# Attention scores by half a chunk at once, with row-half products for the keys' low parts, in a one-core hybrid decoder layer

## The chip, the cores and the metric

The kernel runs on one core of a Trainium2 chip, as one launch. The metric is the device time of that launch in microseconds (us); lower is better. Engines are named as in the profile: PE (matrix products), PEld (its weight loads), DVE (vector), ACT (scalar functions), POOL (GpSimd), SP (issues DMA). PSUM is the memory that products are written to, in eight banks of 512 f32 per partition.

## What is computed

One layer over a new sequence of 4096 tokens and 64 sample tokens, width 1024, all in f32. The parts that matter here:

```python
z = rmsnorm(x, g_pre) @ w_in                       # cut into cb, cc, ch, cg, q, k, v, ag, mq, mg
out_a = silu(cg) * cb * conv3(cc * ch)             # 256 wide
out_b = silu(ag) * window_attention(q, k, v, sink) # 8 query heads, 2 key heads, head_dim 64, window 128
out_c = silu(mg) * attention(mq, mem_k, mem_v)     # 4 heads, head_dim 64, 256 memory tokens
y = concat(out_a, out_b, out_c) @ w_out
x = x + rmsnorm(y, g_post)
```

The window attention goes by blocks of 128 queries against 256 keys (the block before and its own), with one extra sink logit per head. The sample tokens do the same against caches.

## The kernel before

The layer runs in two stages. The first (`input_projection`, up to about 930 us) makes z by Strassen products (line 368) and writes queries, keys, values and gates to DRAM. The second stage computes attention and the output product; the change lies in it.

*High and low parts.* [...] A query tile `q` holds for each head 128 rows: 64 rows of high parts and 64 rows of low parts, in either order. A key tile `kst` holds the high parts of the keys in both halves of its rows (part 0) and the low parts in both halves (part 1). So one product of 128 rows with part 0 gives high x high + low x high, and a second one with part 1 gives the products with the keys' low parts. `mk` holds the memory's keys in the same way.

*Chunks, blocks and units.* Tokens go in 16 chunks of 256, of two 128-token blocks each. `Block.run` (line 1476) makes the output product of one block: two parts of 512 columns, each 8 k-tiles x 3 products (line 1492, tile `y`), so 48 products of 512 columns a block. `starts` names the k at which `start` (line 1525) is called between these products: four times a block from block 2 on, eight times in blocks 0 and 1. Each call puts one unit into PE's stream. A chunk has eight units: four window units (line 1237; one block of queries, one key head, four query heads) and four cross units (line 1174; one head, all 256 queries). Chunk 0 runs in the first stage; chunks 1 and 2 share blocks 0 and 1; from block 2 on a chunk takes two blocks.

*The course of a unit.* A window unit makes 16 score products (line 1246, tile `ws`), ACT copies one half of the scores out (1248), DVE copies the other under a mask (1249), finds maxima (1251), ACT makes exponentials and sums (1259), DVE divides (1264); two calls later PE transposes four heads (1269, tile `wt`), ACT copies them out (1271) and POOL masks them (1276, 1279). A cross unit makes 8 score products (1182, tile `xs`), a maximum (1183), exponentials (1186), one call later POOL multiplies by the reciprocal sums (1191), two calls later PE transposes (1197, tile `xt`) and DVE and ACT copy out one half each (1201). `Pipe.start` (1061) keeps these due times. One call after the transposes of a pair of units PE makes the value products (1088, 1218, 1224, tile `wo`), on column halves of the array and then on quarters of it, and DVE multiplies them into the gates (1227, 1170).

*What sets the order.* The order of this stage is not written out: a planner orders the instructions of each engine from the program's order and its own estimate of when their inputs are there. Each engine runs its queue in that order.

*PSUM.* The eight banks (line 1013) are two each for `s` (scores), `t` (transposes), `z` (y), and one tile of two banks for `pv` (values).

*Loads.* POOL issues four loads of keys (1110) and four of queries (1121) for a chunk, a chunk ahead; SP issues those of gates, x and results. `Block.split` (1460) makes high and low parts of the finished gates on ACT and DVE. Sample tokens are worked in between, in blocks 26 to 28 (`late_start`).

Of the kernel before, what the change touches and what calls it, by code (L numbers as in the profile page):

```python
# [52 lines left out]
def hybrid_layer(ctx: ExitStack, tc: tile.TileContext, a: dict):  # L53
# [951 lines left out]
    def open_attention():  # L1005
# [7 lines left out]
        ps = {tag: ctx.enter_context(tc.tile_pool(name=f"ps{tag}", bufs=1 if tag == "pv" else 2, space=bass.MemoryType.PSUM))  # L1013
              for tag in ("s", "t", "z", "pv")}
# [75 lines left out]
    class Chunk:  # L1090


        def __init__(self, c):
            self.c = c
            self.t0 = NS + CT * c
            self.ts = slice(self.t0, self.t0 + CT)
# [18 lines left out]
        def load_queries(self):  # L1115

            self.q = self.pool("q").tile([P, 12, CT], F32R, tag="q", name=f"q{self.c}")
            for part in range(2):
                for hh in range(2):
                    half = hh if part == 0 else 1 - hh  # L1120
                    G.dma_start(self.q[half * 64 : half * 64 + 64, hh::2, :],  # L1121
                                  qd[part, 1:7, hh * 64 : hh * 64 + 64, self.ts].rearrange("j p n -> p j n"))
# [34 lines left out]
        def cross_pair(self, j, band_values):  # L1157
# [4 lines left out]
            def both():  # L1162
                banks = ps["pv"].tile([P, 2, 512], F32, tag="pv", name=f"wo{c}_{j}") if c else None
# [10 lines left out]
        def cross_unit(self, h, pts):  # L1174
            c, nb = self.c, CT // P
            q = self.q[:, h]
            p = work([P, nb, 256], "p", f"xp{c}_{h}")
            mx, nm, den, rd = (tiny.tile([P, 4], F32, tag=n, name=f"x{n}{c}_{h}") for n in ("mx", "nm", "den", "rd"))
            s = psum("s", f"xs{c}_{h}").rearrange("p (b k) -> p b k", b=nb)
            for i in range(nb):  # L1180
                for part in range(2):
                    TE.matmul(s[:, i, :], q[:, i * P : i * P + P], third["mk"][:, part, h, :], start=part == 0, stop=part == 1)  # L1182
# [4 lines left out]
            V.reciprocal(rd[:, :nb], den[:, :nb])  # L1187
            yield 1
            for i in range(nb):

                G.tensor_scalar(p[:, i, :], p[:, i, :], rd[:, i : i + 1], 0.5, op0=ALU.mult, op1=ALU.mult)  # L1191
            yield 1
            pt = work([P, 2, CT], "xpt", f"xpt{c}_{h}")
            for kt in range(2):
                t = psum("t", f"xt{c}_{h}_{kt}")
# [9 lines left out]
        def window_pair(self, i):  # L1205
# [6 lines left out]
            def both_halves(o):  # L1212
                o = o.rearrange("p a (h q) -> p a h q", h=4)
                for n in range(2):
                    for kvh in range(2):
                        cs = slice(64 * kvh, 64 * kvh + 64)
                        v, p3 = steps[kvh][n]
                        TE.matmul(o[cs, n], v[:, cs], p3[:, :, 64 * n : 64 * n + 64], start=True, stop=False,  # L1218
                                  tile_position=(0, 64 * kvh))
                for n in range(2):  # L1220
                    for kvh in range(2):
                        cs, rs = slice(64 * kvh, 64 * kvh + 64), slice(64 - 64 * n, 128 - 64 * n)
                        v, p3 = steps[kvh][n]
                        TE.matmul(o[cs, 1 - n], v[rs, cs], p3[rs, :, 64 - 64 * n : 128 - 64 * n], start=False, stop=True,  # L1224
                                  tile_position=(64 - 64 * n, 64 * kvh))
                gate = self.mix[:, 4:8, i * P : i * P + P].rearrange("p h (a q) -> p a h q", a=2)
# [298 lines left out]
    def start():  # L1525
# [9 lines left out]
        if n == 0:  # L1535
            chunk_load(c + 1)
# [146 lines left out]
```

## Time and profile before

| what | value |
|---|---|
| median of 3 runs | 1536.71 us (1536.7 to 1536.77) |
| the profiled execution's own time | 1536.4 us |
| its span in the profile | 1534.7 us |
| PE busy | 1521.5 us |
| DVE, ACT, POOL busy | 1145.5, 805.7, 376.1 us |
| first y product, last y product start | 931.2 us, 1528.2 us |
| y products, records and mean length | 1560 of whole blocks, 388 to 399 ns |
| score products of windows (line 1246) | 512, 283 ns |
| transposes of windows (line 1269) | 256, 272 ns |

A record of a PE product lasts from its start to its modelled end. Products overlap in the array, so the pace is the distance from start to start, not the record's length, and a record longer than its usual length shows that the product stood waiting in the array, for its weights for example. The name before the arrow is the tile written, those after it are the tiles read; `128*64` is the part of the array that a product takes (rows times columns). An f32 value product appears as two records.

### The profile page before, as it was taken

Reading aid. Unit: us, or ns where it says so; the run is one execution under the profiler, and the core shown is the slowest. Engines: PE = TensorE matmul, PEld = TensorE weight load, DVE = VectorE, ACT = ScalarE, POOL = GpSimd, SP = SyncE. Lnnn points to the kernel's source line nnn. Section 1 sums busy time; section 2 is a strip of 40 time slices with the busy share of each in tenths; the row PEclk is TensorE's granted clock in tenths of the full one; section 3 lists DMA queues with packets and bytes.
Section 4 is the critical chain, followed back from the end, with each engine's and each line's share of the span. In section 5 each row is a group of like instructions: output and inputs, shape, how many; then the busy total and the mean of one; then the engine's idle time right before and its main releaser. Section 6 shows DMA issues by size and latency. Waiting matters only on the chain.

```text
span 1534.7 us, 30168 instructions
## 1 busy us (share of the span) xinstructions
PE 1521.5 (99%) x11341; PEld 1399.5 (91%) x11341; DVE 1145.5 (75%) x2055; ACT 805.7 (52%) x2039; POOL 376.1 (25%) x603
## 2 busy tenths in 40 slices
PE   9999999999999999999999999999999999999998
PEld 9999999999999999999999998788888888888877
DVE  6788887899988777897777678766666666666743
ACT  6675665475322222354454447655666556565632
POOL 0223332211300000000101203544444444444310
PEclk9999999999999999999999999999999999999999
DMA  9989999878855333677877789977777777777333
GB/s 265 194 222 225 283 284 266 272 242 298 193 181 180 126 126 126 220 230 280 227 273 230 229 293 254 231 161 153 156 148 148 151 162 149 158 160 150 130 110 96
DMA packets 177942, 306.28 MB, mean 200 GB/s; under 512 B 33925, under 2 KB 107653, under 8 KB 177765
## 3 DMA queue, kind: packets, MB, share of 16 engines
q1 hardware_dynamic: 130901, 227.38, 48.2%
q0 software_dynamic: 46176, 75.92, 25.5%
q8 instruction: 90, 1.47, 0.4%
q10 hardware_dynamic: 720, 1.05, 0.2%
q14 instruction: 55, 0.45, 0.1%
HBM read 197.23 MB, written 108.05 MB: 199 GB/s over the span
## 4 chain that ended last, share of the span: by engine, by line
PE 86%; DMA 7%; DVE 4%; issue 1%; ACT 1%; POOL 1%; SPq 0%; ACTq 0%; DVEq 0%; POOLq 0%
PE c L368 47%; PE y L1492 23%; PE ws L1246 4%; DMA nat<-in_x_p 3%; DMA md<-th 2%; PE wo L1088 2%; PE wt L1269 2%; PE xs L1182 2%; PE xt L1197 2%; PE wo L1218 2%; PE wo L1224 1%; PE mem_acc L789 1%; DMA qd<-z 1%; DVE z L375 1%; DMA xr<-in_x_p 0%
## 5 line engine op out<-in xcount | busy, mean ns | idle before, releaser
L1492 PE MATMUL y<-wo,mh 128*128 128x512 f32 (+1 forms) x1040 | 349.8, 399 | 0.0
L375 DVE TENSOR_TENSOR z<-c,z 128x520 f32<-128x520 f32 (+1 forms) x308 | 194.5, 646 | 79.2 <-PE c L368 78.2
L1492 PEld LDWEIGHTS y<-wo,mh 128*128 128x128 f32 x1040 | 194.3, 188 | 39.2 <-issue 2.4
L1492 PE MATMUL y<-wo,ml 128*128 128x512 f32 (+1 forms) x520 | 201.6, 388 | 0.0
L1259 ACT ACTIVATE sm<-sm,wnm 128x128 f32<-128x128 f32 x256 | 99.5, 390 | 61.0 <-DVE wnm L1253 60.2
L1191 POOL TENSOR_SCALAR xp<-xp,xrd 128x256 f32<-128x256 f32 x128 | 74.4, 588 | 209.6 <-DVE xrd L1187 209.6
L1492 PEld LDWEIGHTS y<-wo,ml 128*128 128x128 f32 x520 | 98.2, 189 | 16.3
L1183 DVE TENSOR_REDUCE xmx<-xs 128x2 f32<-128x512 f32 x64 | 44.1, 689 | 59.2 <-PE xs L1182 59.1
L1271 ACT COPY wpt<-wt 128x512 f32<-128x512 f32 x64 | 37.3, 582 | 88.1 <-PE wt L1269 85.6
L1246 PEld LDWEIGHTS ws<-kst,q 128*128 128x128 f32 x512 | 69.9, 190 | 5.3 <-ACT xp L1186 0.7
L1499 DVE TENSOR_TENSOR yn<-y,gpost 128x512 f32<-128x512 f32 (+1 forms) x66 | 45.1, 683 | 39.6 <-PE y L1492 39.3
L1246 PE MATMUL ws<-kst,q 128*128 128x256 f32 x512 | 73.0, 283 | 0.4 <-ACT xp L1186 0.4
L1500 ACT ACTIVATE y<-y 128x512 f32<-128x512 f32 (+1 forms) x66 | 38.6, 584 | 64.2 <-DVE yn L1499 64.2
L737 POOL CAST wmask<-negs 128x256 uint8<-128x256 f32 x1 | 0.9, 864 | 268.3 <-ACT z L377 268.3
L1279 POOL TENSOR_SCALAR_AFFINE_SELECT wpt<-wpt 128x512 f32<-128x512 f32 x64 | 52.7, 824 | 42.1 <-ACT wpt L1271 39.1
L1186 ACT ACTIVATE xp<-xs,xnm 128x256 f32<-128x256 f32 x128 | 58.8, 464 | 7.1 <-DVE xnm L1184 7.1
L1121 POOL DMA_DIRECT2D q<-qd x64 | 42.8, 674 | 70.6 <-DVE wo L186 60.9
L276 ACT ACTIVATE nat<-nat 104x1024 f32<-104x1024 f32 x40 | 42.3, 1057 | 26.1 <-DMA nat<-in_x_p 26.1
L1510 DVE SCALAR_TENSOR_TENSOR xr<-yn,yst,xr 128x1024 f32<-128x1024 f32 (+2 forms) x34 | 43.4, 1280 | 15.5 <-POOL yst L1506 13.2
L1110 POOL DMA_DIRECT2D kst<-qd x64 | 38.6, 616 | 63.5 <-PE xt L1197 41.4
L1249 DVE COPY_PREDICATED sm<-wmask,ws 128x256 f32<-128x256 uint8 x124 | 52.2, 437 | 2.5 <-ACT sm L1248 2.1
L1276 POOL TENSOR_SCALAR_AFFINE_SELECT wpv<-wpt 128x512 f32<-128x512 f32 x62 | 40.2, 648 | 50.6 <-ACT wpt L1271 50.5
(961 smaller groups left out, 5095.5 us busy)
## 6 DMA issues: line engine op xcount, KB each, us to landing
q<-qd POOLq DMA_DIRECT2D x64, 384.0 KB, 7.9
xr<-in_x_p SPq DMA_DIRECT2D x32, 512.0 KB
nat<-in_x_p SPq DMA_DIRECT2D x39, 416.0 KB
o_yp<-xr SPq DMA_DIRECT2D x31, 512.0 KB
md<-th POOLq DMA_DIRECT2D x48, 260.0 KB, 7.9
qd<-zh SPq DMA_DIRECT2D x48, 260.0 KB
qd<-z SPq DMA_DIRECT2D x48, 260.0 KB
kst<-qd POOLq DMA_DIRECT2D x60, 192.0 KB, 5.6
```

The costliest lines, as they stand in the source:

```text
L368: TE.matmul(bank[:, :HW], l, r, start=first and i == 0, stop=last and i == 3 * KH - 1)
L375: add = lambda dst, other: V.tensor_tensor(dst, c, other, op=ALU.add)
L1183: V.tensor_reduce(mx[:, :nb], s, axis=AX.X, op=ALU.max)
L1186: S.activation(p[:, i, :], s[:, i, :], AF.Exp, bias=nm[:, i : i + 1], scale=SCALE, accum_out=den[:, i : i + 1])
L1191: G.tensor_scalar(p[:, i, :], p[:, i, :], rd[:, i : i + 1], 0.5, op0=ALU.mult, op1=ALU.mult)
L1246: TE.matmul(s3[:, hh, :], self.q[:, 4 + 2 * (2 * half + hh) + kvh, i * P : i * P + P], self.kst[:, 2 * kvh + part, i * P : i * P + 2 * P], ...
L1249: V.copy_predicated(sm[:, 2 * half : 2 * half + 2, :], third["wmask"], third["negs"] if first else s3[:, :, 0:P])
L1259: S.activation(sm[:, hh, :], sm[:, hh, :], AF.Exp, bias=nm[:, hh : hh + 1], scale=SCALE, accum_out=den[:, hh : hh + 1])
L1279: G.affine_select(p3, p3, pattern=[[0, 4], [1, P]], compare_op=ALU.is_ge, fill=0.0, base=0, channel_multiplier=-1)
L1492: TE.matmul(acc, self.hl[l][:, k], wo[k][c0 // 512][:, r, c0 % 512 : c0 % 512 + c1 - c0], start=j == 0, stop=j == passes * KT - 1)
L1499: V.tensor_tensor(yn[:m, c0:c1], acc[:m], gpost[:m, c0:c1], op=ALU.mult)
L1510: V.scalar_tensor_tensor(self.xr[:m, cs], yn[:m, cs], st[:m, 3:4], self.xr[:m, cs], op0=ALU.mult, op1=ALU.add)
```

## The change

From chunk 3 on, attention goes by halves of a chunk (one block of queries for the windows, two of the four cross heads for all 256 queries) in place of units:

- `scores(i)` makes all scores of a half at once, 12 products of 128 rows with the keys' high parts. Then come the 12 with the keys' low parts, which now take only the 64 rows of the query's high parts, in pairs: the tiles' two banks have their queries' high parts in the upper or in the lower 64 rows, so that one of a pair takes the upper half of the array's rows and the other the lower half. (The product of the two low parts is no longer made there.) Softmax follows, with one ACT copy and one masked DVE copy per key head where there were two, and POOL's multiplication right behind.
- `transposes(i)` transposes all of a half, with the two window heads in the two banks of one tile and the two cross heads in those of another; one copy of 512 per cross head where there were two of 256.
- `products(i)` makes the value products of a half; they themselves are as before.
- In a block from 3 on, scores come at k = 2 of the first part, products of the half before at k = 2 of the second part and transposes at k = 6 of it. Chunks 1 and 2 still run by units, in blocks 0 to 2.
- PSUM is dealt anew: two tiles of two banks (`w`: window scores, window transposes, values), one of two banks (`x`: cross scores and transposes), two of one bank (`z`: y). Chunks 1 and 2 and the sample tokens take these too.
- A chunk's queries are loaded by eight loads where there were four, so that the order of high and low rows fits; those of the cross heads have rows of 512 bytes.

```diff
-        ps = {tag: ctx.enter_context(tc.tile_pool(name=f"ps{tag}", bufs=1 if tag == "pv" else 2, space=bass.MemoryType.PSUM))
-              for tag in ("s", "t", "z", "pv")}
+        ps = {tag: ctx.enter_context(tc.tile_pool(name=f"ps{tag}", bufs=n, space=bass.MemoryType.PSUM))
+              for tag, n in (("w", 2), ("x", 1), ("z", 2))}
...
-        if tag == "pv":
-
-            return ps[tag].tile([P, 2, 512], F32, tag=tag, name=name)[:, 0]
-        return ps[tag].tile([P, 512], F32, tag=tag, name=name)
+        if tag == "z":
+            return ps[tag].tile([P, 512], F32, tag=tag, name=name)
+        return two_banks("x" if tag == "t" else "w", name)[:, 0]
+
+    def two_banks(tag, name):
+        return ps[tag].tile([P, 2, 512], F32, tag=tag, name=name)
...
+            heads = lambda part, j, ts: qd[part, j : j + 2, :, ts].rearrange("j (v d) n -> d j v n", v=2)
             for part in range(2):
-                for hh in range(2):
-                    half = hh if part == 0 else 1 - hh
-                    G.dma_start(self.q[half * 64 : half * 64 + 64, hh::2, :],
-                                  qd[part, 1:7, hh * 64 : hh * 64 + 64, self.ts].rearrange("j p n -> p j n"))
+                for n in range(2):
+
+                    r = slice(64 * (n ^ part), 64 * (n ^ part) + 64)
+                    G.dma_start(self.q[r, 4 + 4 * n : 8 + 4 * n, :].rearrange("p (j v) n -> p j v n", v=2),
+                                heads(part, 3 + 2 * n, self.ts))
+                    G.dma_start(self.q[r, 0:4, n * P : n * P + P].rearrange("p (j v) n -> p j v n", v=2),
+                                heads(part, 1, slice(self.t0 + n * P, self.t0 + n * P + P)))
...
+            ss = None if self.c == 0 else two_banks("w", f"ws{b}_{kvh}")
             for half in range(2):
-                s = psum("s", f"ws{b}_{kvh}_{half}")
+                s = psum("s", f"ws{b}_{kvh}_{half}") if self.c == 0 else ss[:, half]
...
+        def scores(self, i):
+            c, b, nb = self.c, 2 * self.c + i, CT // P
+            w = [two_banks("w", f"ws{b}_{kvh}") for kvh in range(2)]
+            x = two_banks("x", f"xs{c}_{i}")
+            tasks = []
+            for kvh in range(2):
+                for j in range(4):
+                    tasks.append((w[kvh], j // 2, j % 2, self.q[:, 4 + 2 * j + kvh, i * P : i * P + P],
+                                  lambda part, kvh=kvh: self.kst[:, 2 * kvh + part, i * P : i * P + 2 * P]))
+            for hh in range(2):
+                for n in range(nb):
+                    tasks.append((x, n, hh, self.q[:, 2 * i + hh, n * P : n * P + P],
+                                  lambda part, hh=hh: third["mk"][:, part, 2 * i + hh, :]))
+            for t, bank, col, q, k in tasks:
+
+                TE.matmul(t[:, bank, 256 * col : 256 * col + 256], q, k(0), start=col == 0, stop=True, skip_group_check=col > 0)
+            for t, bank, col, q, k in sorted(tasks, key=lambda x: (x[0] is x, w.index(x[0]) if x[0] in w else 2, x[2], x[1])):
+                r = slice(64 * bank, 64 * bank + 64)
+                TE.matmul(t[:, bank, 256 * col : 256 * col + 256], q[r], k(1)[r], start=False, stop=True,
+                          skip_group_check=True, tile_position=(64 * bank, 0))
+            self.sms, self.ps_ = [], []
+            for kvh in range(2):
+                sm = work([P, 4, P], "sm", f"sm{b}_{kvh}")
+                s4, sm4 = w[kvh].rearrange("p a (h k) -> p a h k", h=2), sm.rearrange("p (a h) k -> p a h k", a=2)
+                S.copy(sm4, s4[:, :, :, P : 2 * P])
+                V.copy_predicated(sm4, third["wmask"].unsqueeze(1).to_broadcast([P, 2, 2, P]), s4[:, :, :, 0:P])
+                self.window_softmax(b, kvh, sm)
+                self.sms.append(sm)
+            for hh in range(2):
+                self.ps_.append(self.cross_softmax(2 * i + hh, x[:, :, 256 * hh : 256 * hh + 256]))
+
+        def transposes(self, i):
+            c, b, nb = self.c, 2 * self.c + i, CT // P
+            self.steps, self.pts = [[], []], [[], []]
+            tw = two_banks("w", f"wt{b}")
+            for kvh in range(2):
+                self.window_transposes(b, kvh, self.sms[kvh], tw[:, kvh], self.steps[kvh])
+            tx = two_banks("x", f"xt{c}_{i}")
+            for hh in range(2):
+                pt = work([P, 2, CT], "xpt", f"xpt{c}_{2 * i + hh}")
+                for kt in range(2):
+                    for n in range(nb):
+                        TE.transpose(tx[:, hh, kt * CT + n * P : kt * CT + n * P + P], self.ps_[hh][:, n, kt * P : kt * P + P], ident)
+                    self.pts[hh].append(pt[:, kt])
+                (S.copy if hh else V.tensor_copy)(pt, tx[:, hh].rearrange("p (a n) -> p a n", a=2))
+            if i == 0:
+                t = two_banks("w", f"vtp{c}")
+                for n in range(2):
+                    self.value(n, t[:, 0, n * P : n * P + P])
...
+    def starts_of(b):
+        if b < 2:
+            return {(p, k): start for p in range(2) for k in (0, 2, 4, 6)}
+        if b == 2:
+            return {(0, 0): start, (0, 2): start, (0, 4): start, (0, 6): lambda: half(6, "scores")}
+        at = {(0, 2): lambda: half(b + 4, "scores"), (0, 6): lambda: None, (1, 2): lambda: half(b + 3, "products"),
+              (1, 6): lambda: half(b + 4, "transposes")}
+        if b == 3:
+            at[0, 0] = lambda: half(6, "transposes")
+        return at
```

`window_transposes` and `window_softmax` are the second and first part of the old window unit, `cross_softmax` and `cross_factors` those of the old cross unit, and `products` calls the old value products with a tile of `w`.

More of the change, by code (lines that the diff above doesn't have):

```diff
@@ L1474, in split, with run @@
             self.hl = [hi, lo]
[L1476 removed]
+        def run(self, last, split, starts):
             b, m = self.b, self.m
@@ L1538, in start, with half, run @@
             chunks[c + 1].load_mix()
-    def run(i, start, starts=(2, 6)):
+    def half(h, what):
+        c, i = divmod(h, 2)
+        if 3 <= c < NCH:
+            getattr(chunks[c], what)(i)
+            if what == "scores":
+                follow(c, 4 * i)
+    def starts_of(b):
[8 more added lines that the diff above has]
+        return at
+    def run(i, starts):
         def split():
```

106 lines of the change are left out of this document (66 added, 40 removed).

## Prediction

> **What bounds the kernel now.** I read the page first: engines, then the chain that ended last.
>
> ```profile
> span 1534.7 us, 30168 instructions
> ...
> PE 1521.5 (99%) x11341; PEld 1399.5 (91%) x11341; DVE 1145.5 (75%) x2055; ACT 805.7 (52%) x2039; POOL 376.1 (25%) x603
> ...
> PE 86%; DMA 7%; DVE 4%; issue 1%; ACT 1%; POOL 1%; SPq 0%; ACTq 0%; DVEq 0%; POOLq 0%
> ```
>
> TensorE (PE) carries 86% of the chain. The change lies in the attention and output stage, from 931 us on, so the second view is the busy time in stretches of that stage, and the third is what PE waited for in it.
>
> ```profile
> core 0: us, PE busy (x) PEld busy (x) DVE busy (x) ACT busy (x) POOL busy (x), PEclk, DMA share, GB/s
> 1020.65:1387.82 367.17, 367.17 (x2261) 300.15 (x2260) 247.29 (x620) 217.60 (x801) 167.48 (x261) 1.00 0.77 155
> 931.22:984.02 52.80, 50.37 (x318) 39.03 (x317) 42.56 (x115) 36.12 (x146) 28.81 (x49) 1.00 1.15 274
> ```
> ```profile
> PE wt L1269 <- DVE xrd L1187: 1.7, 1, 1.7
> PE ws L1246 <- ACT xp L1186: 0.4, 1, 0.4
> PE wt L1269 <- DVE sm L1264: 0.2, 1, 0.2
> ```
>
> The first stretch is 20 blocks of the steady part: 18.36 us each, PE busy throughout, at the full clock. The second is blocks 0 and 1, where two chunks of attention are pressed into two blocks; PE is idle for 2.4 us there. From 931 to 1425 us PE waited for another engine three times, 2.3 us in all. So DVE, ACT, POOL and DMA cost nothing in the steady part, and a change is worth what it does to PE's own stream, plus each wait that it puts into that stream. PE's stream is read from PE's timeline, where the start of one group to the start of the next is the true pace (busy times overlap):
>
> ```profile
> 1200.14 0.39 PE L1492 MATMUL y<-wo,ml 128*128 128x512 f32 x1
> ...
> 1201.52 0.39 PE L1492 MATMUL y<-wo,ml 128*128 128x512 f32 x1
> ...
> 1205.62 1.11 PE L1246 MATMUL ws<-kst,q 128*128 128x256 f32 x8
> 1206.57 0.60 PE L1197 MATMUL xt<-ident,xp 128*128 128x128 f32 x4
> 1206.93 0.48 PE L1492 MATMUL y<-wo,mh 128*128 128x512 f32 x1
> ...
> 1213.93 0.63 PE L1182 MATMUL xs<-mk,q 128*128 128x256 f32 x4
> 1214.49 1.08 PE L1088 MATMUL wo<-xpt,mkv 128*64 128x256 f32 x8
> 1215.41 0.60 PE L1218 MATMUL wo<-wpv,vt 128*64 128x256 f32 x4
> 1215.84 0.60 PE L1218 MATMUL wo<-wpt,vt 128*64 128x256 f32 x4
> 1216.37 0.43 PE L1224 MATMUL wo<-wpv,vt 64*64 64x256 f32 x2
> 1216.38 0.43 PE L1224 MATMUL wo<-wpt,vt 64*64 64x256 f32 x2
> 1216.64 0.38 PE L1224 MATMUL wo<-wpv,vt 64*64 64x256 f32 x2
> 1216.65 0.38 PE L1224 MATMUL wo<-wpt,vt 64*64 64x256 f32 x2
> 1216.96 0.66 PE L1269 MATMUL wt<-ident,sm 128*128 128x128 f32 x4
> ```
>
> A y product takes 1.38/6 = 0.23 us, a score product 0.95/8 = 0.119. Four transposes take 0.36 to the next start, and the y after them has a record of 0.48 instead of 0.39, so 0.45 in truth, 0.11 each.
>
> **The change part by part.** All terms are against the profiled execution's own 1536.4 us (span 1534.7); the median of the runs is 1536.71, 0.3 more.
>
> *Products with the keys' low parts.* Chunks 3 to 15 are 26 halves. Each had 24 score products (16 window, 8 cross) on the whole array. Now 12 stay whole, and 12 take 64 rows each, two at a time on the two row halves. The L1224 rows show tiles of 64 rows and 64 columns, both row halves at once: eight records start in two sets of four, 0.27 apart, and take 0.59 in all, where the eight L1218 records on whole rows (two column halves at once) take 0.96. So row halves do overlap when their results go to different banks, as here. A pair then costs what one product does, 0.119, and I take 0.12. Bounds: 0.12, and 0.24 (no overlap). Removed: 312 x 0.119 = 37.1. Added: 156 x 0.12 = 18.7. Net -18.4, bounds -18.4 and 0.
>
> *Changes of the array's shape.* Whole array to column halves: from xs to wo is 0.56 where four products take 0.48, and the first wo group then takes 0.92 where eight records of L1218 take 2 x 0.43; so 0.08 + 0.06 = 0.14. Column halves to quarters: 0.53 against 0.43, plus 0.27 against 0.215 for the first set, 0.155. The weights of these are 64 columns. Back to a y product directly is seen once:
>
> ```profile
> 954.26 0.38 PE L1224 MATMUL wo<-wpt,vt 64*64 64x256 f32 x2
> 954.57 0.50 PE L1492 MATMUL y<-wo,mh 128*128 128x512 f32 x1
> ```
>
> 0.31 against 0.215, and a record of 0.50 against 0.39: 0.20, because 128 columns of weights lie bare. Row halves have 128 columns too: 0.20 in and 0.20 out, 52 x 0.20 = +10.4 (bounds 52 x 0.14 = 7.3 and 52 x 0.25 = 13). The value products are now followed by y and not by a transpose: 26 x 0.05 = +1.3. In the order of the built kernels, PE's stream from the first y on has 96 changes among whole array, column halves, quarters and row halves before and 168 after. 52 are those above. Of the other 20 all but two lie in blocks 2 and 3, where the planner now splits value products and row-half products into pieces between y products: 20 x 0.17 = +3.4 (0, if PE would have waited there anyway, to 4).
>
> *Banks dealt anew.* Before, every transposed head had a PSUM tile of its own. Now one tile of two banks holds two heads, and as built the waits go by tile: the second window head's transposes wait for ACT's copy of the first out of the other bank, and the second cross head's for DVE's copy. This wait is new, and the whole of PE's stream stands behind it. Its length:
>
> ```profile
> 1217.71 0.59 ACT L1271 COPY wpt<-wt 128x512 f32<-128x512 f32 x1 [0.56 <-PE wt L1269]
> ```
> ```profile
> 960.49 0.92 POOL L1191 TENSOR_SCALAR xp<-xp,xrd 128x256 f32<-128x256 f32 x2
> ```
> ```profile
> 961.02 0.33 PE L1197 MATMUL xt<-ident,xp 128*128 128x128 f32 x1
> ...
> 961.30 0.27 PE L1197 MATMUL xt<-ident,xp 128*128 128x128 f32 x1
> ```
>
> The group of four wt transposes at 1216.96 is through at 1217.62 and its last one, a record of 0.27, starts near 1217.35. ACT copies from 1217.71 to 1218.30, and PE follows a release by about 0.06 (the first xp of two ends near 960.96), with 0.055 more for bare weights (record 0.33 against 0.27). From the start of that last transpose to the next head's first: 1.06. As built, PE has 0.11 + four xt transposes 0.44 + one y 0.23 = 0.78 of work to put there, in the even halves also a value transpose, 0.89. It stands for 0.28 or 0.17, mean 0.22; 24 clean halves: +5.3. Bounds 0 (the copy is hidden) and 24 x 0.5 (ACT busy when the copy is due) = 12. The cross wait is longer cover: DVE's copy of 512 starts at about the same distance and the second window head stands between, so 0.
>
> *The first chunks.* Chunks 1 and 2 still run by units, but scores and values share two tiles and transposes have one tile where they had two banks. Some 30 waits for a copy are new in blocks 0 to 2, and DMA is full there (share 1.15). The planner puts y products into them. I take +2; 0 to 8.
>
> *Hidden at no cost.* POOL issues 8 query loads per chunk for 4: at 0.67 that is 2.7 us of the 36.7 of a chunk.
>
> ```profile
> L1121 POOL DMA_DIRECT2D q<-qd x64 | 42.8, 674 | 70.6 <-DVE wo L186 60.9
> ```
>
> POOL is busy 167 of 367 us, the loads are issued a chunk ahead, and the steady DMA share is 0.77; 512 more packets a chunk leave room. If the cover went, scores would wait for queries; I see no sign. Fewer, larger ACT and DVE copies save time on engines that PE does not wait for.
>
> Sum: -18.4 + 10.4 + 1.3 + 3.4 + 5.3 + 2 = **+4.0**, 1540.4 us, and 1540.7 on the scale of the median. I say 1540.5.
>
> **Rivals.** (B) *PE stays full.* The planner's fillers cover the copies and the pieces in blocks 2 and 3 fall where PE had idled: 2.4 us is there to be filled. Then -18.4 + 11.7 + 1 to 3 = about -4.5, **1532**. For it: PE waited for nothing in 367 us before. Against it: 0.78 of cover for a 1.06 wait. It decides at a copy that comes back 0.22 us sooner or one more y product between.
>
> (C) *The pair does not overlap*, so the change doesn't do what it says. Weight loads are the suspect: one takes 190 ns, 0.11 of it bare when nothing hides it, and a pair needs two. If they came one after another a pair would take 0.24 and the term would be 0: +22, **1558**. Against it: the four L1224 tiles of a set start within 0.02 us of each other, and whole-array scores load and multiply at 0.119 together. [...]
>
> (D) *The softmax of half a chunk is late.* All of a half's scores come at once, and PE wants the first cross transposes about 13.9 us after it begins them (scores 2.5, 18 y, 6 y, values 2.6, 12 y, one window head).
>
> ```profile
> L1259 ACT ACTIVATE sm<-sm,wnm 128x128 f32<-128x128 f32 x256 | 99.5, 390 | 61.0 <-DVE wnm L1253 60.2
> ...
> L1183 DVE TENSOR_REDUCE xmx<-xs 128x2 f32<-128x512 f32 x64 | 44.1, 689 | 59.2 <-PE xs L1182 59.1
> ...
> L1186 ACT ACTIVATE xp<-xs,xnm 128x256 f32<-128x256 f32 x128 | 58.8, 464 | 7.1 <-DVE xnm L1184 7.1
> ...
> L1249 DVE COPY_PREDICATED sm<-wmask,ws 128x256 f32<-128x256 uint8 x124 | 52.2, 437 | 2.5 <-ACT sm L1248 2.1
> ```
>
> Worked by hand: DVE free of the block before at 3.4, two masked copies 1.4, two reductions 1.3, a small one: 6.2; eight exponentials of 0.39 and two short ones on ACT: 9.7; two of 0.46: 10.7; the square of y: 11.3; two more of 0.46, whose maximum DVE has by 12: 13.1. These must be through before the one tile for cross is free for transposes: 0.8 us to spare on 13.9. If the chain is 1.3 us longer, each half loses 0.5: 24 x 0.5 = +12 on the forecast, **1552**.
>
> **How the numbers follow.** Two parts in a thousand, 3.1 us, is about what a measurement of this kernel can tell from no change. Forecast (1536 to 1545): 0.48, of which 0.20 lies within that bound of 1536.7 and 0.28 above it. B: 0.28, of which 0.23 is faster and 0.05 the same. C: 0.08. D: 0.16. So faster 0.23, same 0.25, slower 0.52. The range goes from 1531, the middle of B less a microsecond, to 1551, which leaves out C and the upper half of D, and the lowest part of B.
>
> **What would show it.** In PE's timeline after: pairs of row-half products starting together, 0.12 apart from the next pair (0.24: C); 0.2 about each such group; a gap of 0.2 to 0.3 ahead of the second wt group of a half, released by ACT's wpt copy (none: B); a wait of xt on ACT or POOL xp instead (D). The steady block should take 18.3 to 18.4 us as before; blocks 0 to 3 about 5 us longer in sum. I am wrong if the steady block is under 18.15 or over 18.6, or if blocks 0 to 3 are not longer.

## The result, and the profile after

The changed kernel takes **1554.95 us** (median of 4 runs, 1552.71 to 1558.65) where the kernel before took 1536.7 in the same session: a ratio of **1.0123**, with a 95% interval of 1.0102 to 1.0144. So it is slower, by 18 us. The forecast of 1540.5 had the sign, but the time lies above its range (1531 to 1551).

The page of the changed kernel's profiled execution (1555.6 us) shows where to look. The chain that ended last runs through PE for 74% where it was 86%, and through DMA and DVE for more than before:

```profile
span 1553.9 us, 30124 instructions
PE 1530.5 (98%) x11341; PEld 1379.3 (89%) x11341; DVE 1144.5 (74%) x1977; ACT 797.8 (51%) x1961; POOL 397.8 (26%) x667
PE 74%; DMA 11%; DVE 7%; issue 3%; ACT 3%; POOL 2%; SPq 0%; DVEq 0%; ACTq 0%; POOLq 0%
```

The busy time in the two stretches that the prediction used, the 20 steady blocks and blocks 0 and 1 (first column: stretch and length; PEclk is the granted clock):

```profile
1036.93:1403.10 366.17, 365.30 (x2262) 284.39 (x2260) 247.67 (x560) 210.69 (x742) 174.01 (x305) 1.00 0.77 156
932.63:984.66 52.03, 47.03 (x264) 34.58 (x263) 35.00 (x91) 28.32 (x108) 25.81 (x45) 0.93 1.12 265
```

The steady blocks take 18.31 us each (18.36 before). In blocks 0 and 1 PE now idles 5.0 us, and the clock there is 0.93 on the mean. That stretch is no longer than before (52.0 against 52.8 us), but it holds less work, 264 of PE's records where it held 318; the rest is made up in blocks 2 and 3. And what PE waited for from the first y product to block 25:

```profile
PE xs L1204 <- DVE sm L1270: 4.4, 1, 4.4
PE xt L1353 <- POOL xp L1196: 0.8, 1, 0.8
PE xt L1353 <- issue: 0.5, 2, 0.3
PE xt L1214 <- POOL xp L1196: 0.5, 1, 0.5
PE ws L1267 <- ACT xp L1187: 0.4, 1, 0.4
PE wt L1296 <- ACT wpt L1298: 0.3, 1, 0.3
```

One wait of 4.4 us makes most of it, and it is in the part that still runs by units. The best measure of place is the length of a block, from its first y product to that of the next (48 products), read from PE's timeline. The table has all kernels of this study; their edits follow below.

| kernel | first y at | blocks 0 to 3 | mean of 4 to 25 | blocks 26 to 28 |
|---|---|---|---|---|
| before | 931.2 | 13.3 + 39.5 + 18.2 + 18.4 = 89.4 | 18.36 | 19.5 + 19.9 + 19.2 = 58.6 |
| after | 932.6 | 14.5 + 37.6 + 29.5 + 22.8 = 104.3 | 18.30 | 18.4 + 26.2 + 18.2 = 62.8 |
| e1, transposes in own tiles | 935.8 | 104.8 | 18.24 | 62.1 |
| e2, low products on the whole array | 930.6 | 104.1 | 18.61 | 63.6 |
| e3, old banks for chunks 1 and 2 | 928.7 | 14.3 + 38.1 + 19.0 + 20.4 = 91.8 | 18.29 | 61.7 |
| e4, own buffer for zs_lo | 931.6 | 107.9 | 18.28 | 19.6 + 21.3 + 18.2 = 59.2 |
| e5, x rows later on DVE | 927.7 | 14.5 + 32.2 + 27.5 + 22.4 = 96.6 | 18.29 | 63.1 |
| e6, units with the new banks | 928.7 | 14.5 + 38.1 + 28.3 + 19.2 = 100.1 | 19.15 | 61.0 |
| e7, e3 and e4 together | 927.4 | 14.3 + 51.2 + 19.0 + 20.4 = 104.9 | 18.29 | 59.2 |
| e8, e7 and e1 | 927.5 | 105.1 | 18.24 | 60.0 |
| e9, e7 with two DVE additions held in place | 930.8 | 91.7 | 18.29 | 59.2 |
| e10, e9 and e1 | 930.0 | 95.1 | 18.24 | 60.0 |

From block 29 to the start of the last y product all take the same 45.0 us. The start of the first y product moves between 927 and 936 us although no kernel changes the first stage, so a single execution's total carries some microseconds of that, and block lengths don't. But a block's length is also from one execution, and a late transfer or a slowed clock in it can make 1 to 3 us (in e3's block 27 and e10's block 1, below). Before to after: +1.4 at the first y, +14.9 in blocks 0 to 3, 22 x -0.054 = -1.2 in the steady blocks, +4.3 in blocks 26 to 28: together the 19.2 us between the two profiled executions, within 0.2.

**The stall in block 1.** PE's timeline of the changed kernel (start, length, what; in brackets the idle time before and its releaser):

```profile
953.53 0.40 PE L1580 MATMUL y<-wo,ml 128*128 128x512 f32 x1
958.34 1.22 PE L1204 MATMUL xs<-mk,q 128*128 128x256 f32 x4 [4.41 <-DVE sm L1270]
959.49 1.11 PE L1090 MATMUL wo<-xpt,mkv 128*64 128x256 f32 x2
960.54 1.22 PE L1580 MATMUL y<-wo,mh 128*128 128x512 f32 x2
```

and DVE's at the same time:

```profile
956.65 1.28 DVE L1598 SCALAR_TENSOR_TENSOR xr<-yn,yst,xr 128x1024 f32<-128x1024 f32 x1 [5.18 <-DMA xr<-in_x_p]
957.85 0.76 DVE L1270 COPY_PREDICATED sm<-wmask,ws 128x256 f32<-128x256 uint8 x2
```

The scores `xs` need a `w` tile. Both are taken; one is released by the masked copy at 957.85. That copy stands in DVE's queue behind the last step of block 0, which waits 5.18 us for the rows of x. In the kernel before the same step waited for the same transfer and ran at almost the same time, 956.28, after 2.26 us of waiting:

```profile
956.28 1.63 DVE L1510 SCALAR_TENSOR_TENSOR xr<-yn,yst,xr 128x1024 f32<-128x1024 f32 x1 [2.26 <-DMA xr<-in_x_p]
```

There PE had other work until 958.07, and then stood as well, for DVE's work behind that step, but only 1.72 us:

```profile
959.79 0.63 PE L1269 MATMUL wt<-ident,sm 128*128 128x128 f32 x4 [1.72 <-DVE xrd L1187]
```

So the transfer is hardly later (0.4 us); PE has come to depend earlier on what is queued behind it. After the stall PE's records are long (1.22 for two y products where 0.62 is usual). The stretches around the two long idle times of PE show why:

```profile
953.90:956.88 2.98, 0.03 (x1) 0.00 (x0) 0.23 (x1) 0.00 (x0) 1.26 (x3) 1.00 1.04 394
956.88:963.70 6.82, 5.36 (x15) 3.48 (x17) 5.29 (x15) 3.58 (x19) 0.00 (x0) 0.50 1.26 298
963.70:984.66 20.96, 20.83 (x134) 14.17 (x131) 13.17 (x36) 12.06 (x44) 11.33 (x20) 1.00 1.03 200
1459.90:1462.06 2.16, 0.00 (x0) 0.00 (x0) 0.54 (x2) 0.00 (x0) 1.88 (x7) 1.00 0.00 0
1462.06:1465.46 3.40, 3.12 (x19) 1.64 (x20) 0.58 (x2) 0.00 (x0) 1.17 (x4) 0.50 0.00 0
```

The granted clock is 0.50 from 956.88 to 963.70; PE is busy for 5.36 us of that, and by the longer records I put half of it, 2.7 us, down as lost (an estimate). In block 27 the same follows an idle time of 2.44 us: 3.12 us busy at half the clock, 1.6 lost by the same estimate.

**The wait in block 27.** DVE, POOL and PE there:

```profile
1457.73 0.49 DVE L1399 TENSOR_TENSOR zs<-zs,zs_lo 128x320 f32<-128x320 f32 x1 [1.46 <-DMA zs_lo<-qd]
```
```profile
1458.67 3.12 POOL L1469 COPY skc<-zs 64x64 f32<-64x64 f32 x8
1461.83 0.72 POOL L1417 COPY sq<-zs 64x32 f32<-64x32 f32 x3
```
```profile
1462.34 2.47 PE L1423 MATMUL sms<-sq 128*32 128x256 f32 x16 [2.44 <-POOL sq L1417]
```

The sample tokens' low parts (`zs_lo`) borrow one of the two `sm` buffers. With halves both `sm` buffers are held from the scores to the transposes of a half. So the loads of `zs_lo` start only behind the transposes at 1454.5, DVE adds at 1457.7 (18 us after block 26 begins; in the kernel before at 1430.5, 6 us after), and POOL's copies come too late for the sample scores, which stand ahead of everything else in PE's queue.

### The profile page after: what moved, and what is told of

Same layout as the page of the kernel before. It is cut to its first block, busy times and chain, and to the rows that moved or that the text cites. A ratio compares the mean times of both kernels' runs of the same rounds, so it can differ in the third digit from the quotient of the medians.

```text
span 1553.9 us, 30124 instructions
## 1 busy us (share of the span) xinstructions
PE 1530.5 (98%) x11341; PEld 1379.3 (89%) x11341; DVE 1144.5 (74%) x1977; ACT 797.8 (51%) x1961; POOL 397.8 (26%) x667
## 4 chain that ended last, share of the span: by engine, by line
PE 74%; DMA 11%; DVE 7%; issue 3%; ACT 3%; POOL 2%; SPq 0%; DVEq 0%; ACTq 0%; POOLq 0%
PE c L368 37%; PE y L1580 22%; DMA nat<-in_x_p 3%; DMA md<-th 3%; PE wo L1090 2%; PE wt L1296 2%; PE wo L1246 2%; PE ws L1326 2%; DVE z L375 1%; PE ws L1329 1%; PE wo L1252 1%; PE xt L1353 1%; DMA wr_0A<-in_w_in 1%; PE xs L1326 1%; PE mem_acc L789 1%
## 5 line engine op out<-in xcount | busy, mean ns | idle before, releaser
L1580 PE MATMUL y<-wo,ml 128*128 128x512 f32 (+1 forms) x520 | 205.0, 394 | 0.0
L1196 POOL TENSOR_SCALAR xp<-xp,xrd 128x256 f32<-128x256 f32 x128 | 61.9, 493 | 234.6 <-DVE xrd L1188 232.7
L1187 ACT ACTIVATE xp<-xs,xnm 128x256 f32<-128x256 f32 x128 | 58.9, 464 | 28.1 <-DVE xnm L1185 28.1
L1125 POOL DMA_DIRECT2D q<-qd x64 | 41.4, 647 | 65.1 <-DVE wo L186 59.2
L1335 ACT COPY sm<-ws 128x512 f32<-128x512 f32 x52 | 28.3, 590 | 55.1 <-PE ws L1329 55.1
L1306 POOL TENSOR_SCALAR_AFFINE_SELECT wpt<-wpt 128x512 f32<-128x512 f32 x64 | 45.7, 715 | 39.0 <-ACT wpt L1298 36.8
L407 ACT CAST zh<-z 128x520 fp32r<-128x520 f32 x56 | 33.4, 625 | 33.8 <-DVE z L375 29.5
L377 ACT COPY z<-c 128x520 f32<-128x520 f32 (+1 forms) x44 | 24.4, 554 | 50.2 <-PE c L368 46.9
L1112 POOL DMA_DIRECT2D kst<-qd x64 | 38.8, 617 | 36.4 <-issue 22.4
L1286 ACT ACTIVATION_READ_ACCUMULATOR sm<-sm,wnm 128x1 f32 x256 | 47.8, 187 | 0.0
L1588 ACT ACTIVATE y<-y 128x512 f32<-128x512 f32 (+1 forms) x66 | 38.1, 578 | 18.8 <-DVE yn L1587 18.5
```

The source lines that it names most:

```text
L1125: G.dma_start(self.q[r, 4 + 4 * n : 8 + 4 * n, :].rearrange("p (j v) n -> p j v n", v=2), heads(part, 3 + 2 * n, self.ts))
L1187: S.activation(p[:, i, :], s[:, i, :], AF.Exp, bias=nm[:, i : i + 1], scale=SCALE, accum_out=den[:, i : i + 1])
L1196: G.tensor_scalar(p[:, i, :], p[:, i, :], self.rds[h][:, i : i + 1], 0.5, op0=ALU.mult, op1=ALU.mult)
L1286: S.activation(sm[:, hh, :], sm[:, hh, :], AF.Exp, bias=nm[:, hh : hh + 1], scale=SCALE, accum_out=den[:, hh : hh + 1])
L1306: G.affine_select(p3, p3, pattern=[[0, 4], [1, P]], compare_op=ALU.is_ge, fill=0.0, base=0, channel_multiplier=-1)
L1580: TE.matmul(acc, self.hl[l][:, k], wo[k][c0 // 512][:, r, c0 % 512 : c0 % 512 + c1 - c0], start=j == 0, stop=j == passes * KT - 1)
```

## The experiments

All are edits of the changed kernel. The theory after reading the two traces: (1) the steady part went as forecast; (2) the loss in blocks 0 to 3 comes from the shared two-bank tiles that chunks 1 and 2 now use, mainly through the stall above; (3) the loss at the end comes from the borrowed buffer. The rivals: the passage from units to halves in blocks 2 and 3 costs it, or the row-half products (those with the keys' low parts; a value is the sum of its high and its low part) gain nothing. Each ratio compares an edit's runs with those of the kernel before beside them (median 1534.6 us for e1 to e4, 1533.9 for the others); it is not the quotient of the medians, and the times are not to be held against 1536.7.

### e1: the second window head's wait

```diff
-            tw = two_banks("w", f"wt{b}")
             for kvh in range(2):
-                self.window_transposes(b, kvh, self.sms[kvh], tw[:, kvh], self.steps[kvh])
+                self.window_transposes(b, kvh, self.sms[kvh], two_banks("w", f"wt{b}_{kvh}")[:, 0], self.steps[kvh])
```

> The changed kernel with one edit: the transposes of a half's two window heads go to two tiles of their own instead of to the two banks of one tile, so that the second head need not wait for ACT's copy of the first. Theory (the wait is what the steady part still loses): the gap ahead of the second head, 0.24 us a half in the trace after, goes; the steady block falls from 18.30 to about 18.06 us, the kernel from 1555 to about 1549. Rival (some other wait ends last there, for the next tile or for POOL's multiplication): steady block 18.3, kernel 1555. Blocks 0 to 3 (104.3 us) and 27 (26.2) stay within 1 us in both.

Measured: 1551.58 us, ratio to before 1.0119 (1.0101 to 1.0136). The steady block takes 18.24 us: -0.066 where -0.24 was expected. The gap itself went. In the changed kernel, PE's timeline shows it as forecast:

```profile
1216.42 0.60 PE L1296 MATMUL wt<-ident,sm 128*128 128x128 f32 x4
1216.86 0.60 PE L1353 MATMUL xt<-ident,xp 128*128 128x128 f32 x4
1217.21 0.48 PE L1580 MATMUL y<-wo,mh 128*128 128x512 f32 x1
1217.75 0.66 PE L1296 MATMUL wt<-ident,sm 128*128 128x128 f32 x4
```

The y product's record at 1217.21 is 0.09 longer than usual (0.48 for 0.39), and on PEld's timeline its load of 0.19 starts only at 1217.18; so I put its begin near 1217.30 and the next product's at 1217.53 (estimates). The second head starts at 1217.75, its first load at the same time, and the group of four is longer as well (0.66 for 0.60). Over the 16 halves from 1100 to 1400 us this gap is 0.24 us on the mean. In e1 both heads follow each other as one group of eight:

```profile
1201.24 1.03 PE L1296 MATMUL wt<-ident,sm 128*128 128x128 f32 x8
1202.11 0.60 PE L1352 MATMUL xt<-ident,xp 128*128 128x128 f32 x4
1202.56 0.33 PE L1152 MATMUL vtp<-ident,vT 128*128 128x128 f32 x1
1202.65 0.48 PE L1579 MATMUL y<-wo,mh 128*128 128x512 f32 x1
```

but the records of the value transposes are longer now (0.33; 0.27 in the kernel after), and the second cross head begins 0.06 later behind its y product. Summed over the same stretch these small delays are 0.16 a half. So the theory of the wait holds, and about two thirds of what it costs comes back at the next tiles. On the ratio to the kernel before, 1.0119 against 1.0123, the edit cannot be told from none.

### e2: the row-half products

```diff
-                r = slice(64 * bank, 64 * bank + 64)
-                TE.matmul(t[:, bank, 256 * col : 256 * col + 256], q[r], k(1)[r], start=False, stop=True,
-                          skip_group_check=True, tile_position=(64 * bank, 0))
+                TE.matmul(t[:, bank, 256 * col : 256 * col + 256], q, k(1), start=False, stop=True, skip_group_check=True)
```

> The changed kernel with one edit: the products with the keys' low parts take the whole array again (12 more whole-array products a half where there were 12 on row halves, and no change of shape around them). Theory (pairs run side by side at 0.108 us a pair, and two changes of shape cost 0.41): a half gets 12 x 0.119 - 6 x 0.108 - 0.41 = 0.37 us longer, the steady block 18.67, 26 halves +9.6 us; in block 2 the split row-half pieces go too, which gives some 1 us back: about 1563. Rival (the pairs gain nothing, the whole difference is elsewhere): steady block 18.3, kernel 1553 to 1555.

Measured: 1557.62 us, ratio 1.0154 (1.0138 to 1.0169). The steady block takes 18.61, +0.304, against 0.37 expected and 0 for the rival; the kernel comes out 5 us under the 1563 expected. The pairs do what they should. One such group in the changed kernel:

```profile
1203.01 1.11 PE L1326 MATMUL ws<-kst,q 128*128 128x256 f32 x8
1203.96 0.64 PE L1326 MATMUL xs<-mk,q 128*128 128x256 f32 x4
1204.53 0.74 PE L1329 MATMUL ws<-kst,q 64*128 64x256 f32 x8
1205.11 0.39 PE L1329 MATMUL xs<-mk,q 64*128 64x256 f32 x4
1205.43 0.50 PE L1580 MATMUL y<-wo,mh 128*128 128x512 f32 x1
```

The first eight row-half products take 0.58 to the next start, part of it the change of shape ahead of them. Over the 16 halves from 1100 to 1400 us a pair starts 0.118 us after the pair before it, and not 0.108 as the expectation has it. The change of shape takes 0.19 on the way in and 0.20 on the way out: the next start comes 0.09 later than at the usual pace both times, and the record behind it is 0.10 longer on the way in (0.38 for 0.28) and 0.11 on the way out (0.50 for 0.39). With these a half gets 12 x 0.119 - 6 x 0.118 - 0.40 = 0.32 longer, which is what was measured within 0.02. The weight loads of these pairs are on PEld's timeline:

```profile
1204.52 0.54 PEld L1329 LDWEIGHTS ws<-kst,q 64*128 64x128 f32 x8
```

Each of the eight takes 0.18 to 0.19 us, as long as a load of 128 rows (0.19), and four pairs of them fit into 0.54: the loads of one pair are made while the pair before runs on the same two row halves (the first pair's products are recorded from 1204.53 to 1204.91, the second pair's loads from 1204.63 to 1204.82).

### e3: the banks of chunks 1 and 2

Chunks 1 and 2 take the tiles of the kernel before from pools that are closed when half 6 begins; the shared tiles are opened only then.

```diff
+    def deal_anew():
+        first.close()
+        for tag, n in (("w", 2), ("x", 1)):
+            ps[tag] = ctx.enter_context(tc.tile_pool(name=f"ps{tag}", bufs=n, space=bass.MemoryType.PSUM))
...
-            return {(0, 0): start, (0, 2): start, (0, 4): start, (0, 6): lambda: half(6, "scores")}
+            return {(0, 0): start, (0, 2): start, (0, 4): start, (0, 6): lambda: (deal_anew(), half(6, "scores"))}
```

> The changed kernel with one edit: chunks 1 and 2, which run by units, take the PSUM tiles of the kernel before (single banks for scores and transposes, one tile of two banks for values); the banks are dealt anew only when the halves begin, in block 2. Theory (the shared two-bank tiles tie the units of chunks 1 and 2 to each other's copies: PE stands 4.4 us behind a masked copy of DVE that is queued behind the wait for x, then runs 5 us at half the clock, then works off split pieces): the 4.4 us go, the clock stays 1.0 through blocks 0 and 1, blocks 0 to 3 fall from 104.3 to about 92 us, the kernel to about 1543. Rival (it is the passage from units to halves in blocks 2 and 3 that costs, whatever the banks): blocks 0 and 1 back at 52.8, but blocks 2 and 3 still 50 us; the kernel 1552 or more.

Measured: **1538.73 us**, ratio 1.0038 (1.0024 to 1.0053). Blocks 0 and 1, then 2 and 3, in this kernel:

```profile
928.74:981.19 52.45, 51.63 (x330) 40.25 (x329) 43.91 (x118) 37.62 (x149) 34.84 (x60) 1.00 1.15 281
981.19:1020.52 39.33, 38.02 (x233) 28.78 (x232) 25.00 (x59) 21.41 (x78) 22.39 (x36) 1.00 0.90 168
```

91.8 us together, PE idle for 2.1, full clock: 12.5 of the 14.9 us are gone. The theory's number was 92. What stays is 2.4 us: the passage to halves, the rival's cost, and the eight query loads are in it and not told apart. Block 1 of the kernel before holds its own wait of 1.72 us, which this kernel does not have, so their true price may be nearer 4 (an estimate). The kernel's time lies 4 us under the 1543 expected; in the profiled execution the first y product came 3.9 us earlier, and the clock stayed full in block 27. In the built order the changes of shape in block 2 fall from 22 to 5 as well, so the splitting into pieces was largely a consequence of the shared tiles too.

### e5: the stall alone

Only the place of block 0's last step in DVE's queue changes: it is called in block 1, at k = 5, and held there. The shared tiles stay.

```diff
+            def end_rows():
+                for cs in (slice(0, 512), slice(512, D)) if last else (slice(0, D),):
+                    (tc.keep_in_program_order if b == 0 else lambda x: x)(V.scalar_tensor_tensor(self.xr[:m, cs], yn[:m, cs], st[:m, 3:4], self.xr[:m, cs], op0=ALU.mult, op1=ALU.add))
+                    DMA.dma_start(dst[:, cs], self.xr[:m, cs])
...
+                if b == 1 and p == 0:
+                    starts[0, 5] = ends.pop()
```

> The changed kernel with one edit: the last step of block 0 on DVE (x added to y, line 1598, which waits for x's transfer) is held back by some 45 of DVE's instructions, so that the masked copies of the next scores no longer stand behind it; the shared two-bank tiles stay. Theory (that queue position is what makes PE stand 4.4 us, and the long idle time is what halves the clock): the 4.4 us and the 2.5 us lost at half the clock go, the granted clock is 1.0 in blocks 0 and 1, blocks 0 to 3 fall from 104.3 to about 97.5; about 5 us stay, as pieces and small waits of the shared tiles. Rival 1 (PE would wait for the shared tiles anyway): blocks 0 to 3 stay above 102. Rival 2 (the pieces too only follow from the stall): blocks 0 to 3 fall to 92.

Measured: 1543.37 us, ratio 1.0062 (1.0047 to 1.0076). Blocks 0 and 1, then 2 and 3:

```profile
927.74:974.41 46.67, 45.33 (x268) 33.44 (x266) 36.01 (x93) 28.98 (x111) 28.36 (x46) 1.00 1.29 285
974.41:1024.29 49.88, 48.29 (x294) 34.76 (x294) 33.14 (x84) 30.43 (x115) 30.68 (x51) 1.00 0.92 164
```

96.6 in all against 97.5 expected, and the clock is full. So the stall and the slow clock behind it are 7.8 us of the 14.9, by an edit that touches neither banks nor products.

### e6: the new banks without halves

```diff
-        if n == 0 and c < 3:
+        if n == 0 and c < NCH:
...
-        if c < 3:
+        if c < NCH:
             follow(c, n)
...
+        return {(p, k): start for p in range(2) for k in (2, 6)}
```

> The changed kernel without halves: all chunks go by units as before, with whole-array products, but with the banks dealt anew (two two-bank tiles for scores and values, one for transposes) and the eight query loads. Theory (the banks alone make the loss of blocks 0 and 1): the first stall and the drop of the clock are there as in the changed kernel, blocks 0 to 3 take 97 to 101 us where the kernel before takes 89.4; the steady block 18.36 to 18.5; no wait for the sample tokens in block 27; the kernel 1543 to 1549. Rival (the loss belongs to the passage to halves): blocks 0 to 3 take 90 to 92, the kernel about 1537.

Measured: 1564.34 us, ratio 1.0194 (1.0178 to 1.021). PE's two longest waits from 925 to 1380 us:

```profile
PE xs L1204 <- DVE sm L1270: 4.7, 1, 4.7
PE xt L1214 <- DVE xpt L1218: 4.4, 15, 0.4
```

The stall is there, with no half in the program, and blocks 0 to 3 take 100.1 as the theory said. The steady block is a miss: 19.15 where 18.36 to 18.5 was expected. A cross unit's transposes now wait for the copies of the unit before out of their one tile; the second line shows 4.4 us of that in some 20 blocks, 0.2 of the 0.79 a block, and the rest is not told apart. The banks alone are a loss in the steady part as well; halves are what makes them bearable.

### e4, e7 and e9: the buffer of the sample tokens

```diff
+        third["lo"] = late.tile([P, 7, NS], F32, name="zs_lo")
...
-        zs, lo = third["zs"], work([P, 4, P], "sm", "zs_lo").rearrange("p a n -> p (a n)")[:, : 7 * NS].rearrange("p (a n) -> p a n", n=NS)
+        zs, lo = third["zs"], third["lo"]
```

> The changed kernel with one edit: the low parts of the sample tokens get a buffer of their own instead of one of the two softmax buffers sm. Theory (with halves both sm buffers are held from the scores to the transposes, 14 us, so the sample tokens' loads start only after block 26's transposes, POOL gets to sq only at 1462, and PE stands 2.4 us ahead of the sample scores and then runs about 3 us at half the clock): the wait goes, block 27 falls from 26.2 to about 22, the kernel by 4.2 to about 1551. Rival (POOL is late because of its masks, not because of the buffer): block 27 stays 26. The planner orders blocks 1 to 3 somewhat differently in this kernel too; their sum may move by a few us either way, and is told apart by the blocks' lengths.

Measured: 1549.95 us, ratio 1.0106 (1.0089 to 1.0122). Blocks 26 to 28 fall by 3.6 us and block 27 to 21.3, so the buffer is the cause of most of the 4.3 lost there. Blocks 0 to 3 rise by the same 3.6. DVE makes the additions of the sample tokens at 974.6 us already, in block 1, and the first chunks are ordered differently around them; most of the rise is in block 3 (26.5 for 22.8), where PE stood 1.92 us for POOL's `xp` and the clock was then 0.50 from 1022.60 to 1029.43. Whether the order or the one execution brought that on is open. Together with the old banks:

> Two edits together: the banks of the kernel before for chunks 1 and 2, and the own buffer for the low parts of the sample tokens. Theory (two separate causes): blocks 0 to 3 92, steady block 18.29, blocks 26 to 28 from 61.7 to about 59; 2.5 us under the kernel with the first edit alone, so within 1 us of the kernel before. Rival: the tail stays at 61.7.

Measured: 1548.78 us, ratio 1.0097 (1.008 to 1.0114). The tail is right (59.2), but block 1 takes 51.2. DVE's waits in block 1 name the reason:

```profile
DVE zs L1407 <- DMA zs<-md: 12.8, 1, 12.8
```

Nothing holds the sample tokens' additions back any more, and the planner puts them into DVE's queue some 25 blocks early, ahead of the softmax (by its own estimate, it seems, their transfer is there in time); PE then waits 11.8 us for DVE. e9 holds the two additions at their place and calls for the tokens half a block ahead of block 26:

```diff
-        V.tensor_tensor(zs[:, 0:5], zs[:, 0:5], lo[:, 0:5], op=ALU.add)
+        tc.keep_in_program_order(V.tensor_tensor(zs[:, 0:5], zs[:, 0:5], lo[:, 0:5], op=ALU.add))
...
+        if i == 25:
+            starts[1, 0] = sample_tokens
```

> The kernel with the banks of before in chunks 1 and 2, and the own buffer for the sample tokens' low parts, with DVE's two additions for the sample tokens now held at their place in the program, half a block ahead of block 26 (in the run before, the planner had moved them into block 1, where DVE stood 12.8 us for their transfer). Theory (the own buffer does its work in the tail, and the loss of the run before is that one wait): blocks 0 to 3 91.8 as with the banks alone, blocks 4 to 25 18.29, blocks 26 to 28 about 59.2; 0.999 to 1.002 of the kernel before. Rival (the buffer itself moves the first chunks): blocks 0 to 3 over 95.

Measured: 1537.23 us, ratio **1.0016** (1.0007 to 1.0025). Blocks 0 to 3, 4 to 25 and 26 to 28:

```profile
930.80:1022.51 91.71, 89.65 (x560) 69.03 (x559) 68.60 (x176) 58.99 (x225) 57.14 (x95) 1.00 1.08 235
1022.51:1424.93 402.42, 401.83 (x2487) 313.01 (x2486) 272.96 (x618) 231.63 (x815) 189.65 (x339) 1.00 0.75 155
1424.93:1484.09 59.16, 58.16 (x384) 42.92 (x383) 35.12 (x86) 29.48 (x100) 12.52 (x25) 1.00 0.36 116
```

All three are as expected. Edits that touch no product of the steady part take back nearly all of the loss.

### e8 and e10: everything together

> The two edits and the window heads' transposes in tiles of their own. By the blocks measured one by one: blocks 0 to 3 92 (89.4 before), blocks 4 to 25 18.22 (18.36 before, so 3 us less), blocks 26 to 28 59 (58.6 before): the sum is the time of the kernel before within 1 us, 0.999 to 1.001 of it. If the three edits help each other, 0.997; if one undoes another, 1.003.

Measured: 1551.04 us, ratio 1.0108 (1.009 to 1.0127). It has e7's wait in block 1 (PE stands 12.9 us), so it tells nothing on the sum.

> The same with the window heads' transposes in tiles of their own. From the blocks measured: 91.8 + 22 x 18.24 + 59.5, against 89.4 + 22 x 18.36 + 58.6 before: 0.7 us more and so within 0.998 to 1.002 of the kernel before, some 1.2 us under the run beside it. Rival (the tiles of their own cost in the tail what they gain): equal to the run beside it.

Measured: 1537.01 us, ratio 1.0011 (1.0 to 1.0022). The steady block is 18.24 as in e1. Its profiled execution lost 1.6 us of PE time in block 1, where DVE waited 2.1 us for the rows of x, and 1.7 more at half the clock behind that (961.15 to 964.56), which is why blocks 0 to 3 take 95.1; in e9 DVE waited 0.3 us there, so this part differs between executions. The 1.2 us under e9 did not show: the steady blocks gain 22 x 0.053 = 1.2 on e9, blocks 26 to 28 lose 0.8, and the medians are 0.2 apart, nearer to the rival. No version here beats the kernel before: the best two lie 1 to 2 parts in a thousand above it.

## Why the prediction was wrong

The steady part was right, term by term. Low products: -18.4 + 10.4 = -8.0 for 26 halves, 0.31 each; e2 measured 0.304. A pair costs 0.118 (0.12 forecast), a change of shape 0.19 to 0.20 (0.20). The wait of the second window head was put at 0.22 a half and is 0.24, though by e1 only 0.07 of it can be had back. The whole steady block is 18.30, within the 18.3 to 18.4 forecast. Rival C (no overlap) is excluded by e2: with a pair at 0.24 the edit would have made a half shorter. That the measured time lies within 4 us of C's 1558 is chance. C's suspect, the weight loads, did not hold the pairs up: a pair's two loads (0.18 to 0.19 each) are made while the pair before runs on the same two row halves, and the pairs follow each other at 0.118. Rival D (the softmax of a half is late) is not seen in the steady part; once, for half 6 in block 3, PE waits 0.8 us for POOL's `xp`.

The step that failed is **"The first chunks ... I take +2; 0 to 8"**, with the 3.4 for further changes of shape in blocks 2 and 3 beside it: 5.4 forecast, 14.9 measured, more than the upper bounds of both terms together (8 + 4). By the runs these are 7.8 for the stall and the slow clock behind it (e5), about 4.8 for the rest of what the shared tiles do (what e3 takes away beyond e5: pieces, changes of shape, small waits, not told apart), and 2.4 that stay with the old banks. (That the parts add up is assumed; no run has both edits.) The prediction counted the new waits and took them for short ones that the planner would fill. It priced a wait by the copy that ends it, and did not ask what stands ahead of that copy in DVE's queue. The kernel before showed that as well: DVE's 2.26 us for x at 956.28 stood behind PE's longest wait of the stage, the 1.7 us of `PE wt L1269 <- DVE xrd L1187` in the prediction's own third view. The prediction read its length and did not follow it back.

The second failing step is one that is missing: blocks 26 to 28 have no term, and cost 4.3. The buffer that the sample tokens borrow is held longer by halves; e4 shows that this is the cause of 3.6 of them. Without these two the forecast's own terms give the time: +4.0, less the 5.4 for blocks 0 to 3, is -1.4 for the rest, and the steady blocks gave -1.2.

The signs that the prediction set for being wrong did not catch this: the steady block stayed between 18.15 and 18.6 and blocks 0 to 3 did get longer. Only the size, 14.9 for about 5, showed the fault; the sign had no upper bound.

## What to carry to other kernels

When two buffers become one, each wait on it is priced by the whole queue of the engine that frees it, DMA waits ahead of that instruction included (here 4.41 us of PE behind 5.18 of DVE), and not by the freeing instruction alone; in the old trace, a short wait of the bottleneck engine, followed back through the other engine's queue, shows where such a wait already stands. When an operation holds a buffer longer, look for everyone who borrows that buffer, also far from the change. A change to a steady loop is worth 1 us here and its two ends cost 19, so price the ends first.

## What the runs showed of the hardware

An idle time of PE had a second cost in the changed kernel. Around the end of 4.41 us of idle (953.93 to 958.34) the granted clock was 0.50 for 6.82 us (956.88 to 963.70), and around that of 2.44 us (to 1462.34) for 3.40 (1462.06 to 1465.46); by the estimate above PE lost 2.7 and 1.6 us by that. But the length of the idle time does not sort the cases: the same 2.44 us in e3 and 1.72 us in the kernel before left the clock at 1.00, and behind 1.6 us in e10 it was 0.50 for 3.41 us. The rows are two neighbouring stretches of about 3.4 us in each of the kernel before, e3 and e10, the first of them with the larger part of the idle time (stretch, length, then PE's busy time; the third number from the end is the granted clock):

```profile
956.52:959.94 3.42, 1.70 (x12) 1.36 (x11) 3.42 (x9) 1.17 (x5) 1.36 (x3) 1.00 1.32 280
959.94:963.35 3.41, 3.27 (x25) 2.72 (x24) 2.92 (x10) 2.39 (x10) 3.40 (x7) 1.00 1.26 277
1441.14:1444.55 3.41, 1.98 (x11) 1.51 (x9) 2.51 (x6) 1.66 (x3) 3.14 (x8) 1.00 0.00 0
1444.55:1447.97 3.42, 2.41 (x23) 1.34 (x23) 0.73 (x2) 0.00 (x0) 1.79 (x7) 1.00 0.00 0
957.74:961.15 3.41, 1.31 (x10) 1.03 (x10) 2.42 (x9) 0.96 (x2) 2.62 (x4) 1.00 1.27 277
961.15:964.56 3.41, 3.41 (x19) 3.19 (x17) 2.75 (x7) 2.18 (x9) 3.21 (x7) 0.50 1.10 339
```

In the kernel before, PE was busy for 1.70 us of the first stretch, and in e3, where the idle time falls on both, for 1.98 and 2.41; the clock stayed at 1.00. In e10 PE was busy for 1.31 us, and the stretch behind that was at 0.50. In the changed kernel it was busy for 0.46 us from 953.47 to 956.88 and for 1.26 from 1458.64 to 1462.05, and the clock was 0.50 behind both. These are five cases, their figures change with where a stretch is laid, and the ends of PE's records are modelled; what decides is not shown.
